# Output projection of a hybrid decoder layer by seven block products, with attention's turns spaced by a least amount of other matmuls

## The chip, the cores and the metric

One core of one Trainium2 chip runs the whole program. The time is that of the device, in microseconds (us), the median of the runs of one kernel. The profile and the trace come from one more execution, whose own time stands beside its span in the table below.

## The reference

One layer over 1024 tokens and 1024 channels in fp32: a combined projection, differential attention, an mLSTM, two gated merges, an output projection and a norm. What the change touches is the end:

```python
merged = (jax.nn.sigmoid(ga) * jnp.einsum('bsw,wd->bsd', ya, w_a[l])
          + jax.nn.sigmoid(gb) * jnp.einsum('bsw,wd->bsd', yb, w_b[l]))
out = jnp.einsum('bsd,de->bse', merged, w_out[l])
x = x + _rmsnorm(out, norm_post[l])
```

`ya` is the result of attention (4 heads, 8 query blocks of 128 each, causal), `yb` that of the mLSTM.

## The kernel before

**Precision.** A product of fp32 matrices is done in three passes of the type fp32r. `split` writes each operand as a high half (a copy by ScalarE, ACT, in which the type is narrowed) and a low half (`tensor_sub` on VectorE, DVE), and TensorE (PE) adds high by high, high by low and low by high. A product over 512 rows of depth and 512 columns is 4 times 3 = 12 matmuls of 128x512.

**Seven products in place of eight.** The projections at the start take a pair of column blocks. Inputs and weights are cut in two by two, and `Combos` and `Banks` make the four output blocks out of seven products (`PRODS`, products 0 to 6) of sums and differences of blocks. `pair_steps` gives the order: product 6 of a pair comes after product 0 of the next. `prep` makes the operand two products ahead, `run` issues 12 matmuls and then what follows (`after`): a copy to SBUF by ACT after products 0, 2 and 3, a finished block (`sink`) after products 1, 4, 5 and 6. The output projection does not use this scheme.

**Attention and the fill.** `attn_head` makes, for query block i, the scores (`score`, tile S), the exponentials (L956) and the difference of the two softmaxes (`combine`, L970) on DVE and ACT. In the next turn the result is transposed on PE (`turn`, tile pT), and a turn later weighed (`weigh`, tile pv). Between turns `weave` pulls other matmuls from `fill` (the remaining pairs, then the merge of the mLSTM's half, `merge_b`), six at a time, an amount of 1.4 in its own count. What a turn may pull is the supply over the turns by `share`, and what was pulled too much before is held back, though never below 0.6 of the want.

**Second merge and output projection.** `merge("ma", ...)` runs 16 groups of 12 matmuls (8 blocks d of columns, two halves of the tokens). After each group DVE multiplies by the gate out of PSUM (L1108), adds the other merge's result (L1181), and `split` writes M, high and low. Then come 16 output tiles of 24 matmuls (two column halves `cc`, eight token blocks `tt`). After each tile ACT squares it (L1209) and DVE multiplies by the norm's weights (L1213); in the second half each token block is finished by GpSimd (L1220, L1221), DVE (L1226) and a DMA out (L1230). The raw output weights are loaded and split by `out_weights` between the groups of the merges.

**What sets the order.** Each engine runs its own instructions in a fixed order. A scheduler orders them when the program is built; only the matmuls, up to the end of attention (L1169), are held to the order of the code. All DMAs are issued from SP, in one order. Tiles live in pools with few buffers (`raw` 4, `wc` 3, `st` 5, `tm` 4; PSUM 3 in `acc` and 5 in `misc`), and a tile waits until the last reader of the one before it is done.

Of the kernel before, what the change touches and what calls it, by code (L numbers as in the profile page):

```python
# [9 lines left out]
F32 = mybir.dt.float32  # L10
# [6 lines left out]
P = 128  # L17
# [16 lines left out]
RESERVE = 12.0  # L34
FB = 8
LAST = 5


@with_exitstack
def kernel(  # L40
# [47 lines left out]
    def acc(name):  # L88
        return ps_acc.tile([P, 512], F32, tag="acc", name=name)
# [4 lines left out]
    def slot(i, shape, name, dtype=F32):  # L94
        return tp.tile(shape, dtype, tag=f"T{i}", name=name)
# [7 lines left out]
    def raw_tile(shape, name):  # L103
        return wp.tile(shape, F32, tag="raw", name=f"raw_{name}", bufs=4)
# [4 lines left out]
    def drain(gen):  # L109
        for _ in gen:  # L110
            pass
# [226 lines left out]
    class Banks:  # L338


        def __init__(self, width, name, sink):
            self.w, self.name, self.sink = width, name, sink
            self.b, self.t = {}, {}

        def bank(self, b):
            if b not in self.b:
                self.b[b] = acc(f"{self.name}{b}")[:, 0 : self.w]
            return self.b[b]

        def keep(self, what, b):  # L350
# [684 lines left out]

    left = [0.0]

    def weave(chain):
        for want in chain:
            turns(2)  # L1040
            due = left[0] + want
            now = max(due, 0.6 * want)
            left[0] = pull(now) + due - now

    def until(name):
# [3 lines left out]
        left[0] -= pulled[0] - was  # L1049


    wide, homes = {}, {}

    def out_weights(cc, kh, g):

        if (cc, kh) not in homes:
            tags = {(0, 0): ("t4h", "t4l"), (1, 0): ("t2h", "t2l"), (1, 1): ("t1h", "t1l")}
            if (cc, kh) in tags:
                two = [
                    hp.tile([P, 4, 512], F32R, tag=f"h{t}", name=f"wo{t}") for t in tags[cc, kh]  # L1060
                ]
                homes[cc, kh] = [[two[e][:, n * 2 : n * 2 + 2] for e in range(2)] for n in range(2)]
            else:
                four = [slot(8 + n, [P, 2, 512], f"wo{n}", F32R) for n in range(4)]
                homes[cc, kh] = [four[0:2], four[2:4]]
        dst = homes[cc, kh][g]
        for k in range(2):
            for e in range(2):
                wide[cc, kh, g * 2 + k, e] = dst[e][:, k]
        r = raw_tile([P, 2, 512], f"o{cc}{kh}{g}")  # L1070
        k0 = kh * 4 + g * 2
        nc.sync.dma_start(r, w_out_v[:, k0 : k0 + 2, cc * 512 : cc * 512 + 512])
        split(r, *dst)


    def load_y(slot0, heads, tags):
# [42 lines left out]
    def merge_b():  # L1119
        ys = load_y(4, range(4), ("11h", "11l", "21h", "21l"))  # L1120
        n = 0
        for due in merge("mb", w_b_v, 1, ys, keep_b):
            yield due
            n += 1
            if n in (8, 14):
                out_weights(0, 0, (n - 8) // 6)
            if n == 20:
                ys_a.extend(load_y(0, range(3), YA))
        done.add("mb")
# [39 lines left out]
    ordered[0] = False  # L1169

    M = {}
    for kh in range(2):
        for T in range(2):
            for e in range(2):
                tag = (("t3h", "t3l"), ("22h", "22l"), ("21h", "21l"), ("11h", "11l"))[kh * 2 + T][e]
                M[kh, T, e] = hp.tile([P, 4, 512], F32R, tag=f"h{tag}", name=f"m{kh}{T}{e}")

    def finish_a(d, half, tg):
        mb = part("mb")
        nc.sync.dma_start(mb, m_d[d][:, hs_(half)])  # L1180
        nc.vector.tensor_add(tg, tg, mb)  # L1181
        split(tg, M[d // 4, half, 0][:, d % 4], M[d // 4, half, 1][:, d % 4])

    drain(merge("ma", w_a_v, 0, ys_a, finish_a, (acc, misc)))


    npost = slot(13, [P, D], "npost")
    nc.sync.dma_start(npost, norm_post[0].partition_broadcast(P))
    orow = [slot(i, [P, D], f"o_{i}") for i in range(8)]
    ssq = cp.tile([P, NT, 2], F32, name="ssq")  # L1190

    for cc in range(2):
        for kh in range(2):
            for g in range(2):
                if (cc, kh) != (0, 0):
                    out_weights(cc, kh, g)
        c0 = cc * 512
        for tt in range(NT):
            ts_ = slice(tt * P, (tt + 1) * P)
            js = slice((tt % 4) * P, (tt % 4 + 1) * P)  # L1200
            ps = (misc if tt % 2 else acc)("out")
            for kt in range(KT):
                for i, (a, b) in enumerate(((0, 0), (0, 1), (1, 0))):
                    mm(
                        ps, M[kt // 4, tt // 4, a][:, kt % 4, js], wide[cc, kt // 4, kt % 4, b],
                        start=(kt == 0 and i == 0), stop=(kt == KT - 1 and i == 2),
                    )
            junk = part("oj")
            nc.scalar.activation(  # L1209
                junk, ps, AF.Square, scale=D ** -0.5, accum_out=ssq[:, tt, cc : cc + 1]  # L1210
            )
            orr = orow[tt]
            nc.vector.tensor_mul(orr[:, c0 : c0 + 512], ps, npost[:, c0 : c0 + 512])  # L1213
            if cc == 0:
                nc.gpsimd.tensor_scalar(
                    ssq[:, tt, 0:1], ssq[:, tt, 0:1], 1.0, 4.0 * EPS, ALU.mult, ALU.add
                )
                continue
            st = sp.tile([P, 3], F32, tag="ost", name="ost")
            nc.gpsimd.tensor_add(st[:, 0:1], ssq[:, tt, 0:1], ssq[:, tt, 1:2])  # L1220
            nc.gpsimd.tensor_tensor(st[:, 2:3], st[:, 0:1], mhalf[:, 0:1], ALU.pow)  # L1221
            xr = slot(8 + tt % 4, [P, D], "xr")
            nc.sync.dma_start(xr, x[0, ts_, :])
            for n0 in range(0, D, 512):
                ns = slice(n0, n0 + 512)
                nc.vector.scalar_tensor_tensor(  # L1226
                    out=orr[:, ns], in0=orr[:, ns], scalar=st[:, 2:3], in1=xr[:, ns],
                    op0=ALU.mult, op1=ALU.add,
                )
                nc.sync.dma_start(out[0, ts_, ns], orr[:, ns])  # L1230


_INS = ["x", "norm_pre", "norm_post", "w_in", "b_if", "conv_qk", "lambda_qk",
# [25 lines left out]
```

## Time and profile before

| | |
|---|---|
| median of 3 runs | 843.53 us (843.45 to 843.87) |
| the profiled execution's own time | 841.9 us |
| mean granted clock of PE | 0.999 |

The program in stretches, busy us of each engine (the windows view; the last two stretches stand in the prediction):

| stretch, us | PE | DVE | ACT | DMA share |
|---|---|---|---|---|
| 0 to 40, load and first projections | 38.40 | 30.05 | 24.85 | 0.75 |
| 40 to 375, projections with the mLSTM | 335.00 | 251.09 | 162.58 | 0.41 |
| 375 to 680, attention with fill | 301.86 | 217.27 | 179.45 | 0.54 |
| 680 to 702.3, end of the first merge | 22.30 | 10.56 | 3.64 | 0.65 |

The columns of a timeline row are start, duration, engine, line, operation, out<-in, shape and count; what stands in brackets is idle time ahead of it and what ended it. Matmuls overlap, so a row's duration is not the pace: the pace is the distance of the starts.

### The profile page before, as it was taken

The page shows a single profiled execution, that of the slowest core. Times are in us where ns is not written, and L with a number is a line of the kernel's source. Part 1 is how long each engine was busy: PE and PEld are TensorE (multiplying, and loading weights), DVE is VectorE, ACT ScalarE, POOL GpSimd, SP SyncE. Part 2 cuts the span into 40 slices and gives each one's busy share as a digit, 9 for nine tenths or more (in the row PEclk, how much of TensorE's full clock was granted, in tenths as well). Part 3 has the DMA queues.
Part 4 walks back from the last instruction along what each step waited for, and adds up shares of the span by engine and source line. Part 5 has one row for each costly group of instructions (what it writes and reads, how often), then busy time and mean ns, then how long its engine had stood idle before and what let it go on. Part 6 is the DMA issues. An engine that isn't in the chain of part 4 may idle for free.

```text
span 840.2 us, 12224 instructions
## 1 busy us (share of the span) xinstructions
PE 829.3 (99%) x4282; PEld 706.5 (84%) x4282; DVE 573.0 (68%) x1161; ACT 400.4 (48%) x892; POOL 36.5 (4%) x70
## 2 busy tenths in 40 slices
PE   9999999999999999999999999999999999999997
PEld 7998888888888888888888888788888888888885
DVE  6996969769659767568767875587587734981133
ACT  6663545444544544446655655466576521341110
POOL 1100000000000000010010000000100000000011
PEclk9999999999999999999999999999999999999999
DMA  7712441451542547266256426442666757830252
GB/s 238 216 40 70 101 151 51 138 163 51 176 143 83 174 146 231 89 208 202 92 161 228 126 74 204 139 162 75 224 208 229 271 184 263 295 105 1 101 200 101
DMA packets 100482, 128.44 MB, mean 153 GB/s; under 512 B 8666, under 2 KB 60098, under 8 KB 100420
## 3 DMA queue, kind: packets, MB, share of 16 engines
q1 hardware_dynamic: 100420, 127.66, 47.9%
q8 instruction: 34, 0.56, 0.3%
q14 instruction: 28, 0.23, 0.1%
HBM read 88.27 MB, written 39.35 MB: 152 GB/s over the span
## 4 chain that ended last, share of the span: by engine, by line
PE 95%; DMA 2%; DVE 1%; ACT 1%; issue 1%; SPq 0%; POOL 0%; DVEq 0%; POOLq 0%; ACTq 0%
PE out L80 10%; PE mrg L80 10%; PE tok L80 6%; PE S L80 4%; PE pv L80 4%; PE pT L83 2%; PE num L80 2%; PE qkb0Y L80 1%; PE g04Y L80 1%; PE g00Y L80 1%; PE za1Y L80 1%; PE g12Y L80 1%; PE g02Y L80 1%; PE zb0Y L80 1%; PE za0Y L80 1%; PE g10Y L80 1%
## 5 line engine op out<-in xcount | busy, mean ns | idle before, releaser
L956 ACT ACTIVATE p<-p,ast 128x128 f32<-128x128 f32 (+7 forms) x64 | 49.5, 775 | 31.2 <-DVE ast L955 23.5
L949 DVE CUSTOM_DVE_ANT_0 p<-S,gm 128x384 f32<-128x384 f32 (+5 forms) x96 | 49.8, 554 | 13.4 <-PE S L80 11.7
L1213 DVE TENSOR_TENSOR o<-out,npost 128x512 f32<-128x512 f32 x16 | 11.1, 691 | 57.3 <-ACT oj L1209 57.3
L80 PE MATMUL mrg<-y,mbw 128*128 128x512 f32 x192 | 44.9, 391 | 0.0
L80 PE MATMUL mrg<-y,maw 128*128 128x512 f32 x192 | 43.7, 389 | 0.0
L1209 ACT ACTIVATE oj<-out 128x512 f32<-128x512 f32 x16 | 9.6, 598 | 71.5 <-PE out L80 71.5
L80 PEld LDWEIGHTS mrg<-y,maw 128*128 128x128 f32 x192 | 36.0, 188 | 7.5
L80 PEld LDWEIGHTS mrg<-y,mbw 128*128 128x128 f32 x192 | 35.8, 188 | 7.3
L80 PEld LDWEIGHTS pv<-va,pT 128*128 128x128 f32 x288 | 37.2, 191 | 2.6
L80 PE MATMUL pv<-va,pT 128*128 128x128 f32 x288 | 37.4, 275 | 0.0
L80 PE MATMUL S<-khh,qs 128*128 128x384 f32 (+5 forms) x96 | 34.9, 369 | 0.3 <-ACT pT L986 0.2
L80 PE MATMUL S<-kll,qs 128*128 128x384 f32 (+5 forms) x96 | 32.4, 342 | 0.4 <-DMA kll<-qk_d 0.4
L1108 DVE SCALAR_TENSOR_TENSOR tg<-tg,mrg 128x512 f32<-128x512 f32 x32 | 21.8, 682 | 14.6 <-PE mrg L80 12.9
L754 DVE SCALAR_TENSOR_TENSOR cv<-pad,cols,cv 128x1024 f32<-128x1024 f32 x24 | 30.7, 1280 | 0.2
L970 DVE SCALAR_TENSOR_TENSOR p<-p,ast,p 128x128 f32<-128x128 f32 (+7 forms) x32 | 26.1, 816 | 0.7
L823 ACT ACTIVATE junk<-raw 128x128 bf16<-128x128 f32 x32 | 9.9, 310 | 31.6 <-DVE raw L818 31.4
L80 PE MATMUL out<-wo,m 128*128 128x512 f32 x96 | 23.7, 395 | 0.0
L83 PE MATMUL pT<-ident,p 128*128 128x128 f32 x144 | 21.2, 274 | 2.5 <-DVE p L970 2.5
L986 ACT COPY pT<-pT 128x512 f32<-128x512 f32 (+3 forms) x48 | 21.9, 488 | 2.7 <-PE pT L83 2.5
L80 PEld LDWEIGHTS out<-wo,m 128*128 128x128 f32 x96 | 18.0, 188 | 4.4 <-DVE m L115 0.2
L995 ACT ACTIVATE oa<-pv 128x128 f32<-128x128 f32 x32 | 8.8, 276 | 26.3 <-PE pv L80 26.1
L80 PE MATMUL out<-wot4h,m 128*128 128x512 f32 x64 | 21.1, 390 | 0.0
(1240 smaller groups left out, 2465.4 us busy)
## 6 DMA issues: line engine op xcount, KB each, us to landing
raw_g<-in_w_in_dram SPq DMA_DIRECT2D x16, 512.0 KB, 3.6
g_d<-g SPq DMA_DIRECT2D x32, 256.0 KB, 3.6
tg<-g_d SPq DMA_DIRECT2D x32, 256.0 KB, 3.5
raw_qkb<-in_w_in_dram SPq DMA_DIRECT2D x16, 256.0 KB, 3.2
z_d<-zt SPq DMA_DIRECT2D x16, 256.0 KB, 2.8
zs<-z_d SPq DMA_DIRECT2D x16, 256.0 KB, 4.6
raw_qka<-in_w_in_dram SPq DMA_DIRECT2D x16, 256.0 KB, 3.1
qk_d<-qah SPq DMA_DIRECT2D x16, 256.0 KB, 2.3
```

The source lines that it names most:

```text
L80: pin(nc.tensor.matmul(*args, **kw))
L83: pin(nc.tensor.transpose(out=out, in_=in_, identity=ident))
L754: nc.vector.scalar_tensor_tensor(out=cv, in0=pad[:, t : t + S], scalar=cols[:, t * 8 + blk : t * 8 + blk + 1], in1=cv, op0=ALU.mult, op1=A ...
L823: nc.scalar.activation(junk, raw[:, c, 0:P], AF.Square, accum_out=stbs[h, c // 4][:, 1, c % 4 : c % 4 + 1])
L949: nc.vector.tensor_tensor_reduce(out=pr[:, n0:n1], in0=pss[:, : n1 - n0], in1=gm[:, (7 - i) * P + n0 : (7 - i) * P + n1], scale=-0.125, sc ...
L956: nc.scalar.activation(pr[:, :nk], pr[:, :nk], AF.Exp, bias=nm, scale=-1.0, accum_out=sth[:, c, i : i + 1],)
L970: nc.vector.scalar_tensor_tensor(out=p0[:, :nk], in0=p1[:, :nk], scalar=st[:, 3:4], in1=p0[:, :nk], op0=ALU.mult, op1=ALU.add,)
L986: nc.scalar.copy(pT[:, j0:j1], pt[:, 0 : (j1 - j0) * P].rearrange("p (j t) -> p j t", t=P))
L995: nc.scalar.activation(raw[:, i], pv[:, 0:P], AF.Square, accum_out=sth[:, 2, i : i + 1])
L1108: nc.vector.scalar_tensor_tensor(out=tg, in0=tg, scalar=1.0, in1=ps, op0=ALU.add, op1=ALU.mult)
L1209: nc.scalar.activation(junk, ps, AF.Square, scale=D ** -0.5, accum_out=ssq[:, tt, cc : cc + 1])
L1213: nc.vector.tensor_mul(orr[:, c0 : c0 + 512], ps, npost[:, c0 : c0 + 512])
```

## The change

Three parts.

**The output projection** is done by the seven-product scheme. Four pairs (`OutPair`, p = 0 to 3) take token blocks p and p + 4 and both column halves: 28 products of 12 matmuls in place of 16 tiles of 24. The weights' sums and differences (t1 to t4) and their halves are made by `wo_first` in steps between the groups of the second merge, the halves of block 22 and of t4 inside the first four products. M is kept in fp32 (`finish_a` adds straight into it), its combinations and halves are made per product by `prep`. A token block is finished (`finish_row`) as soon as both of its column halves are done, so during the products and not in a second pass.

**Attention's turns.** `weave` gets a least amount (CHAIN = 5.2) for attention: a turn pulls at least that much, or its whole want where that is less, whatever was pulled too much before.

**One pull of 2.5** ahead of the first head.

```diff
-    def weave(chain):
+    def weave(chain, least=0.0):
         for want in chain:
             turns(2)
             due = left[0] + want
-            now = max(due, 0.6 * want)
+            now = max(due, 0.6 * want, min(want, least))
             left[0] = pull(now) + due - now
...
     flip_half(*before[0], 7, 1)
+    pull(2.5)
...
-        weave(attn_head(h, stk, gm, supply, before if h else None, after, res))
+        weave(attn_head(h, stk, gm, supply, before if h else None, after, res), CHAIN)
...
     def finish_a(d, half, tg):
         mb = part("mb")
         nc.sync.dma_start(mb, m_d[d][:, hs_(half)])
-        nc.vector.tensor_add(tg, tg, mb)
-        split(tg, M[d // 4, half, 0][:, d % 4], M[d // 4, half, 1][:, d % 4])
+        nc.vector.tensor_add(M[d // 4, half][:, d % 4], tg, mb)
...
+    def wo_first(g):
+        b11, b12, b22, b21 = (
+            wo_load(kh, cc, g, home)
+            for kh, cc, home in ((0, 0, 10), (0, 1, 11), (1, 1, 12), (1, 0, 8 + g))
+        )
+        yield
+        wo_split("11", g, b11)
+        yield
+        nc.vector.tensor_sub(b12, b12, b11)
+        wo_split("t1", g, b12)
...
+    for n, _ in enumerate(merge("ma", w_a_v, 0, ys_a, finish_a, (acc, misc))):
+        if n % 2 and n > 2:
+            next(wo_steps, None)
...
+    class OutPair:
...
+        def early(self):
+            js = slice(self.p * P, self.p * P + P)
+            s2 = part(f"os2_{self.p}").rearrange("p (k c) -> p k c", k=4)
+            self.cb = Combos(M[0, 0][:, :, js], M[1, 0][:, :, js], M[0, 1][:, :, js], M[1, 1][:, :, js], s2)
...
+    for n, (p, i) in enumerate(steps):
+        if n + 2 < len(steps):
+            q, i2 = steps[n + 2]
+            outs[q].prep(i2)
+        if n == 0:
+            wo_home("22", ("t2h", "t2l"))
+            wo_home("t4", ("t1h", "t1l"))
+        if n in (0, 1):
+            wo_split("22", n, wo_load(1, 1, n))
+        if n in (2, 3):
+            wo_split("t4", n - 2, t4_raw[n - 2])
+        outs[p].run(i)
```

How the orders change, at three places. **PE, start of attention's third head**, before: from the last scores of block 0 (S) to their transpose (pT); qka3 is a projection pair of the fill.

```order
L80 MATMUL S<-kll_2_5258,qs_2_5254 128x128
L80 MATMUL qka3Y<-ht2h,qka3w_5315 128x512
L80 MATMUL qka3Y<-ht2l,qka3w_5315 128x512
L80 MATMUL qka3Y<-ht2h,qka3w_5315 128x512 x2
L80 MATMUL qka3Y<-ht2l,qka3w_5315 128x512
L80 MATMUL qka3Y<-ht2h,qka3w_5315 128x512
L80 MATMUL qka3Z<-ht1h,qka3w_5361 128x512
L80 MATMUL qka3Z<-ht1l,qka3w_5361 128x512
L80 MATMUL qka3Z<-ht1h,qka3w_5361 128x512 x2
L80 MATMUL qka3Z<-ht1l,qka3w_5361 128x512
L80 MATMUL qka3Z<-ht1h,qka3w_5361 128x512
L83 MATMUL pT<-ident,p_5415 128x128
```

The same engine and turn now; between the S rows and the first of these stand four more matmuls of qka3Z.

```order
L81 MATMUL qka3Z<-ht1l,qka3w_5361 128x512
L81 MATMUL qka3Z<-ht1h,qka3w_5361 128x512
L81 MATMUL qka3Y<-ht3h,qka3w_5397 128x512
L81 MATMUL qka3Y<-ht3l,qka3w_5397 128x512
L81 MATMUL qka3Y<-ht3h,qka3w_5397 128x512 x2
L81 MATMUL qka3Y<-ht3l,qka3w_5397 128x512
L81 MATMUL qka3Y<-ht3h,qka3w_5397 128x512 x2
L81 MATMUL qka3Y<-ht3l,qka3w_5397 128x512
L81 MATMUL qka3Y<-ht3h,qka3w_5397 128x512 x2
L81 MATMUL qka3Y<-ht3l,qka3w_5397 128x512
L81 MATMUL qka3Y<-ht3h,qka3w_5397 128x512
L84 MATMUL pT<-ident,p_5434 128x128
```

18 matmuls stand between scores and transpose, where there were 12. **DVE, from the last groups of the second merge (tg<-tg,mrg) into the output projection**, before:

```order
L1108 SCALAR_TENSOR_TENSOR tg<-tg,mrg 128x512
L1181 TENSOR_TENSOR tg<-tg,mb 128x512
L115 TENSOR_TENSOR wot2l<-raw_o_7594,wot2h 128x1024
L1108 SCALAR_TENSOR_TENSOR tg<-tg,mrg 128x512
L115 TENSOR_TENSOR m_6966<-tg,m_6965 128x512
L1181 TENSOR_TENSOR tg<-tg,mb 128x512
L115 TENSOR_TENSOR wot2l<-raw_o_7598,wot2h 128x1024
L115 TENSOR_TENSOR m_6968<-tg,m_6967 128x512
```

The same place now; the two tg<-tg,mrg are again the last two groups, m_6953 and m_6954 are the lower halves of M in depth, ow is the operand of a product, os its combination s2, wo22 and wot4 are halves of the output weights.

```order
L1140 SCALAR_TENSOR_TENSOR tg<-tg,mrg 128x512
L1209 TENSOR_TENSOR m_6953<-tg,mb 128x512
L116 TENSOR_TENSOR wo22l<-raw_o_7371,wo22h 128x1024
L1140 SCALAR_TENSOR_TENSOR tg<-tg,mrg 128x512
L116 TENSOR_TENSOR ow_7359<-m_6953,ow_7359 128x512
L1209 TENSOR_TENSOR m_6954<-tg,mb 128x512
L116 TENSOR_TENSOR wo22l<-raw_o_7394,wo22h 128x1024
L329 TENSOR_TENSOR os_0_7352<-m_6954,m_6952 128x512
L116 TENSOR_TENSOR wot4l<-o_7014,wot4h 128x1024
L116 TENSOR_TENSOR ow_7362<-os_0_7352,ow_7362 128x512
```

The operand of product 1 (ow_7359) stands right behind the last group, that of product 2 (ow_7362) five instructions further, two of them of 128x1024. **DVE, end of pair 0**, before: a token block in the second pass of the projection.

```order
L1213 TENSOR_TENSOR o_7339<-out,npost 128x512
L1226 SCALAR_TENSOR_TENSOR o_7339<-o_7339,ost,xr 128x512 x2
L1213 TENSOR_TENSOR o_7340<-out,npost 128x512
L1226 SCALAR_TENSOR_TENSOR o_7340<-o_7340,ost,xr 128x512 x2
```

Now, from the sink of product 5 of pair 0 to the sink of product 6:

```order
L1253 TENSOR_TENSOR o_7411<-out_u_7434,out0Z 128x512
L116 TENSOR_TENSOR ow_7506<-m_6953,ow_7506 128x512
L329 TENSOR_TENSOR os_1_7353<-m_6954,m_6952 128x512
L1258 TENSOR_TENSOR o_7411<-o_7411,npost 128x512
L1238 SCALAR_TENSOR_TENSOR o_7411<-o_7411,ost,raw_xr_7500 128x512 x2
L334 TENSOR_TENSOR m_6951<-os_1_7353,m_6951 128x4x128
L116 TENSOR_TENSOR ow_7524<-os_1_7353,ow_7524 128x512
L336 TENSOR_TENSOR m_6953<-m_6953,os_1_7353 128x4x128
L1258 TENSOR_TENSOR o_7472<-out0Y,npost 128x512
L1238 SCALAR_TENSOR_TENSOR o_7472<-o_7472,ost,raw_xr_7547 128x512 x2
```

Operands of pair 1 now stand between the sinks of pair 0, behind instructions that wait for products and for GpSimd.

More of the change, by code (lines that the diff above doesn't have):

```diff
@@ L36 @@
 LAST = 5
+CHAIN = 5.2
 @with_exitstack
@@ L1049, in until @@
         left[0] -= pulled[0] - was
[L1052 to L1070, printed above, removed]
+    WO = {}
@@ new lines, in wo_home, with wo_slots, wo_split @@
+    def wo_home(name, tags):
+        two = [hp.tile([P, 4, 512], F32R, tag=f"h{t}", name=f"wo{name}{e}") for t, e in zip(tags, "hl")]
+        WO[name] = [[two[e][:, g * 2 : g * 2 + 2] for g in range(2)] for e in range(2)]
+    def wo_slots(name, first_):
+        WO[name] = [
+            [slot(first_ + e * 2 + g, [P, 2, 512], f"wo{name}{e}{g}", F32R) for g in range(2)]
+            for e in range(2)
+        ]
+    def wo_split(name, g, raw):
+        split(raw, WO[name][0][g], WO[name][1][g])
@@ L1187 @@
+    drain(wo_steps)
     npost = slot(13, [P, D], "npost")
     nc.sync.dma_start(npost, norm_post[0].partition_broadcast(P))
-    orow = [slot(i, [P, D], f"o_{i}") for i in range(8)]
     ssq = cp.tile([P, NT, 2], F32, name="ssq")
[L1192 to L1207, printed above, removed]
+    orow, ocount = {}, {}
@@ L1217 @@
                 )
[L1218 to L1230, printed above, removed]
+            else:
+                finish_row(tt)
```

101 lines of the change are left out of this document (86 added, 15 removed).

## The prediction

> **What bounds the kernel now.** I read the page's busy times and chain first, then the chain in order of time, then the waits of PE.
>
> ```profile
> span 840.2 us, 12224 instructions
> ...
> PE 829.3 (99%) x4282; PEld 706.5 (84%) x4282; DVE 573.0 (68%) x1161; ACT 400.4 (48%) x892; POOL 36.5 (4%) x70
> ...
> PE 95%; DMA 2%; DVE 1%; ACT 1%; issue 1%; SPq 0%; POOL 0%; DVEq 0%; POOLq 0%; ACTq 0%
> ```
>
> PE is busy nearly throughout and is 95% of the chain: a matmul less is time less, as long as DVE and ACT keep up. The chain in order of time ends with these rows; the first is a single product of the projections:
>
> ```profile
> 482.79 2.72 PE qka2Y L80 x12
> ...
> 691.82 54.43 PE mrg L80 x240
> 746.25 87.83 PE out L80 x384
> ```
>
> A matmul of 128x512 takes 2.72/12 = 0.227 us in a product and 54.43/240 = 0.227 in the merge; the output projection runs at 87.83/384 = 0.229. It holds 87.83 us and nothing else is in its chain. Whether the other engines have room is read from the windows of the second merge and of the projection:
>
> ```profile
> core 0: us, PE busy (x) PEld busy (x) DVE busy (x) ACT busy (x) POOL busy (x), PEclk, DMA share, GB/s
> 702.30:746.10 43.80, 43.80 (x195) 36.25 (x195) 32.80 (x50) 13.32 (x21) 0.00 (x0) 1.00 0.79 263
> 746.10:834.10 88.00, 87.97 (x385) 71.81 (x383) 29.17 (x41) 15.88 (x37) 7.02 (x22) 1.00 0.25 90
> ```
>
> In the projection DVE has 59 us free; in the merge 11, and the change loads both.
>
> **The projection's matmuls.** 28 products of 12 replace 384 matmuls. At 2.72 us, a few at 2.73, they take 76.3 us, so 87.83 - 76.3 = **11.5 us** go. The operands that PE reads are still halves of type fp32r (the rows ow, wo), so I keep the pace. The Trainium skill ("TensorE: Matmul & The Clock Gate", Back-to-back issue gap) gives about 131 ns as the sustained distance of matmuls with 512 columns; by it the 48 matmuls that go would be worth 6.3 us. The trace's own 227 ns speaks against it, and the measurement decides.
>
> **Attention.** The waits view gives PE two real waits there, and the timeline shows the first as start to start:
>
> ```profile
> PE pT L83 <- DVE p L970: 2.5, 2, 1.5
> PE S L80 <- DMA kll<-qk_d: 0.4, 1, 0.4
> ```
>
> ```profile
> 541.41 0.28 PE L80 MATMUL S<-kll,qs 128*128 128x128 f32 x1
> ...
> 544.10 0.39 PE L80 MATMUL qka3Z<-ht1h,qka3w 128*128 128x512 f32 x1
> 545.94 0.30 PE L83 MATMUL pT<-ident,p 128*128 128x128 f32 x1 [1.45 <-DVE p L970]
> ...
> 550.35 0.47 PE L80 MATMUL qka3Y<-ht3h,qka3w 128*128 128x512 f32 x1
> 551.85 0.44 PE L83 MATMUL pT<-ident,p 128*128 128x128 f32 x2 [1.02 <-DVE p L970]
> ```
>
> From 544.10 to 545.94 PE did one matmul of 0.23: 1.6 us lost; from 550.35 to 551.85, 1.3. The busy view hides 0.2 of each, since ends are modelled. In the new order 18 matmuls stand where 12 did, 1.36 us more, which leaves some 0.2 of the first wait; the second gets at least as much and goes. That is 2.7 us. The kll wait gets 2.8 us of matmuls (the pull of 2.5) ahead of it: up to 0.4 more. Against it, turns late in a head now pull four sixes where they pulled up to six. The longest chain of such a turn, block 7 of head 0:
>
> ```profile
> 421.37 0.48 PE L80 MATMUL S<-khh,qs 128*128 128x512 f32 x1
> ...
> 423.07 0.39 PE L80 MATMUL S<-kll,qs 128*128 128x512 f32 x1
> ...
> 428.74 1.28 DVE L970 SCALAR_TENSOR_TENSOR p<-p,ast,p 128x1024 f32<-128x1024 f32 x1
> ...
> 431.49 1.73 PE L80 MATMUL pv<-va,pT 128*128 128x128 f32 x14
> ...
> 433.05 1.04 PE L83 MATMUL pT<-ident,p 128*128 128x128 f32 x8
> ```
>
> The scores end at 423.3 and p at 430.0, 6.7 us; PE used 9.7 us there. Four sixes and the seven weighings (431.49 to 433.05, 1.56) now give 24 x 0.227 + 1.56 = 7.0 us: just enough here, too little where DVE is held by other work. I take 0.5 us for such turns, between 0 and 2.9, today's two waits coming back. Attention: **-2.6 us**, between -3.1 and +0.2.
>
> **The hand-over to the projection.** DVE's durations, and ACT's casts:
>
> ```profile
> L1108 DVE SCALAR_TENSOR_TENSOR tg<-tg,mrg 128x512 f32<-128x512 f32 x21 | 14.3, 681 | 5.7 <-PE mrg L80 4.5 <-DMA tg<-g_d 1.2
> L1226 DVE SCALAR_TENSOR_TENSOR o<-o,ost,xr 128x512 f32<-128x512 f32 x16 | 11.3, 748 | 1.8 <-POOL ost L1221 1.8
> L115 DVE TENSOR_TENSOR m<-tg,m 128x512 fp32r<-128x512 f32 x16 | 11.0, 690 | 4.7 <-ACT m L114 4.1
> L1181 DVE TENSOR_TENSOR tg<-tg,mb 128x512 f32<-128x512 f32 x16 | 11.0, 687 | 0.2
> L115 DVE TENSOR_TENSOR wo<-raw_o,wo 128x1024 fp32r<-128x1024 f32 x2 | 2.5, 1225 | 4.7 <-ACT wo L114 4.7
> ...
> L114 ACT CAST m<-tg 128x512 fp32r<-128x512 f32 x16 | 9.9, 622 | 23.1 <-DVE tg L1181 23.0
> ```
>
> Fp32 M saves DVE 16 x 0.69 = 11 us in the merge; against it come 18 instructions of 128x1024 at 1.22 (five halves and four differences for each of two parts), 22 us, of which some five run ahead of it. From the merge's first group to its last the new order has 15 multiplies, 15 adds, 11 others of 128x512 and 12 of 128x1024 on DVE. Back to back, starts are 0.08 less apart than durations (746.85 to 747.46 below for 0.69): 41 x 0.61 + 12 x 1.14 = 39 us, against 15 x 2.72 = 40.8 on PE. That leaves no room to catch up once DVE is late, and it is late today:
>
> ```profile
> 711.85 1.23 DVE L115 TENSOR_TENSOR wo<-raw_o,wo 128x1024 fp32r<-128x1024 f32 x1 [4.66 <-ACT wo L114]
> ...
> 746.85 0.69 DVE L115 TENSOR_TENSOR m<-tg,m 128x512 fp32r<-128x512 f32 x1 [0.69 <-ACT m L114]
> 747.46 0.68 DVE L1108 SCALAR_TENSOR_TENSOR tg<-tg,mrg 128x512 f32<-128x512 f32 x1
> ...
> 749.92 0.68 DVE L1108 SCALAR_TENSOR_TENSOR tg<-tg,mrg 128x512 f32<-128x512 f32 x1
> ```
>
> The merge's matmuls end at 746.3, DVE takes up the last group at 749.9: 3.6 us late since a load of weights held it for 4.7. Today that costs PE nothing. In the new order, with DVE late by L, the operand of product 2 is ready L + 5.4 after PE ends the merge (multiply, low half, add, weights 1.14, combination, weights 1.14, low half: 5 x 0.62 + 2 x 1.14), and PE wants it, after two products and two matmuls, at 5.9. The weights of the second half are again loaded late (slot 10 comes free only when the first half is used). I take L = 3: **+2.5 us**, between 0 (L up to 0.5) and 5 (L = 5.5, half more than today).
>
> **Inside the pairs.** Per pair DVE does 11 instructions for operands, 3 adds and 4 multiplies at 0.69 and 4 of L1226 at 0.75: 15.4 us, and PE takes 7 x 2.72 = 19.0. After each finished block DVE waits for ACT's square and GpSimd, today's rows at the end showing 1.6 us from the square to L1226, of which the multiply covers 0.7: 15.4 + 2 x 0.9 = 17.2. That fits; **+0.3 us** for single late operands, between 0 and 2.
>
> **The end.**
>
> ```profile
> 831.13 6.43 SPq L1230 DMA_DIRECT2D out_dram<-o  x4
> ...
> 833.68 0.39 PE L80 MATMUL out<-wot1h,m 128*128 128x512 f32 x1
> ...
> 834.17 0.60 ACT L1209 ACTIVATE oj<-out 128x512 f32<-128x512 f32 x1 [4.75 <-PE out L80]
> ...
> 835.79 1.41 DVE L1226 SCALAR_TENSOR_TENSOR o<-o,ost,xr 128x512 f32<-128x512 f32 x2 [0.21 <-POOL ost L1221]
> ```
>
> The block before the last now ends one product, 2.7 us, before the end instead of 5.5; its L1226 still stands ahead of the last multiply: **+0.2 us**, between 0 and 1.
>
> **Sum.** -11.5 - 2.6 + 2.5 + 0.3 + 0.2 = **-11.1 us**. The profiled execution took 841.9 (span 840.2 and 1.7 around it), so its like would take 830.8. The median of the runs is 843.53, 1.6 above it; from there I predict **832.4 us**.
>
> **Rivals.**
>
> *The hand-over holds PE for long.* For it: DVE at 39 of 40.8 us, and 4.7 us lost today to one load. With 5 us there instead of 2.5 the time is 835. And PE has a slow pace, seen at the start of the program:
>
> ```profile
> 14.93 1.08 PE L80 MATMUL tok<-wc,h21l 128*128 128x264 f32 x4
> 15.81 0.83 PE L80 MATMUL tok<-wc,h21h 128*128 128x264 f32 x4
> 16.48 0.64 PE L80 MATMUL tok<-wc,h11h 128*128 128x256 f32 x4
> 16.96 0.27 PE L83 MATMUL xT<-ident,x 128*128 128x128 f32 x1
> ```
>
> Four matmuls of 264 columns took 0.88 us until 15.8, four of 256 then 0.48: nearly double pace. If a wait threw PE back to the slow pace for some 12 matmuls, 12 x 0.23 = 2.7 us come on top: 837.6, in round numbers 838. Against it: the product behind the wait that ends at 551.85 keeps its pace.
>
> ```profile
> 554.13 2.73 PE qka3Z L80 x12
> ```
>
> The clock gate of the Trainium skill ("TensorE: Matmul & The Clock Gate", What's actually happening) halves the clock after an idle window of about 3.4 us; no wait of PE in this trace is so long after the start, so the runs so far cannot show it. **15%, 838.**
>
> *The waits of attention move.* Late turns have less cover: by the upper bound above +0.2 instead of -2.6, so 835. For it: 7.0 us of cover against a chain of 6.7. Against it: the same turns then also hold less of the fill's DVE work. **12%.**
>
> *DVE paces the pairs: slower than before.* Its FIFO puts each operand behind a sink. Today the low half of M waits 0.69 us for its cast in many groups (the row with 4.7 idle). If all 7 operands of a pair waited so, and all 4 sinks 0.9, a pair takes 15.4 + 4.8 + 3.6 = 23.8 us, and the projection 95.2 + 2.5 against 87.8: 851. It ends slower than today from 22.6 us a pair (3.5 more than PE's 19.0, 14 us in four pairs). Against it: the order puts operands two products ahead, so casts mostly run beside other DVE work. **5%.**
>
> *The products do not save what they should*, because matmuls lose pace with new tiles: nothing in the order speaks for it; 843.5. **2%.**
>
> *Everything fits*: -11.5 for the matmuls, -3.1 in attention, no late hand-over: 829. **7%.**
>
> **How the numbers follow.** My forecast has 59%; its own range is 830 to 835. The range for 8 in 10 is 828.5 to 838.5: left out are the DVE rival, the one without a saving and the far ends of the others. A measurement of this kernel tells about 0.2% from no change. Faster by more: 59 + 15 + 12 + 7 = 93%; within: 2%; slower: 5%.
>
> **What would show it.** The chain's rows of out3 should end about 76 us plus waits after the second merge; out rows x336 at 0.227. PE's waits for p L973 should be below 1 us in sum, and those late in heads show whether they moved. At the hand-over, the distance from the last merge matmul to the last multiply on DVE is L, and gaps of PE before products 1 and 2 are its price. I am wrong if PE's gaps inside the pairs exceed 2 us, if the merge itself waits for weights, or if attention's gaps are as large as before.

## The result, and the profile after

The changed kernel takes **833.0 us** (median of 4 runs, 832.1 to 834.2) where the kernel before, in the runs beside it, took 843.5: a ratio of 0.9891, with a 95% interval of 0.9877 to 0.9904. Measured once more later, beside other kernels, it stood at 0.9861 (0.9835 to 0.9887). The profiled execution took 832.5 us where that of before took 841.9, so 9.4 less. The ratios below, though not the medians, leave out one of nine executions of the kernel with two more multiplies per product: the profiled one, which took 2747 us, so that this kernel has no usable profile.

The page of the changed kernel, the rows that answer to those of before (span, busy time by engine, shares of the chain that ended last):

```profile
span 830.8 us, 12221 instructions
...
PE 817.1 (98%) x4234; PEld 696.6 (84%) x4234; DVE 613.6 (74%) x1215; ACT 420.5 (51%) x922; POOL 45.8 (6%) x70
...
PE 83%; DVE 6%; DMA 5%; issue 3%; ACT 1%; SPq 1%; POOL 0%; DVEq 0%; ACTq 0%; POOLq 0%
```

48 matmul records are gone, PE is busy 12.2 us less and DVE 40.6 us more, and PE's share of the chain has dropped from 95% to 83%: DVE and DMAs now end last in places. That is not a measure of lost time, as PE is still busy 98% of the span. Where PE stood still, its waits say (what waited and for what, us in all, times, the longest; waits of the program's start left out):

```profile
PE pT L84 <- DVE p L973: 1.6, 1, 1.6
...
PE qka1Z L81 <- ACT qka_p L355: 1.1, 1, 1.1
PE mrg L81 <- DVE maw L116: 1.0, 1, 1.0
...
PE out0Y L81 <- ACT ow L115: 0.4, 1, 0.4
...
PE out0Y L81 <- DVE ow L116: 0.3, 1, 0.3
...
PE mrg L81 <- DVE tg L1140: 0.2, 1, 0.2
```

The two waits for p of before (2.5 us) and the one for kll (0.4) are gone. In their place stand two others in attention, and two inside the merges (mrg), for which the prediction's sum has no term.

The hand-over, in the timeline of the changed kernel:

```profile
734.86 10.72 PE L81 MATMUL mrg<-y,maw 128*128 128x512 f32 x46 [0.96 <-DVE maw L116]
745.42 0.39 PE L81 MATMUL out0Y<-wo11h,ow 128*128 128x512 f32 x1
...
747.46 0.68 DVE L1140 SCALAR_TENSOR_TENSOR tg<-tg,mrg 128x512 f32<-128x512 f32 x1
...
751.84 0.50 PE L81 MATMUL out0Y<-wot2h,ow 128*128 128x512 f32 x1 [0.45 <-ACT ow L115]
752.13 0.68 DVE L116 TENSOR_TENSOR ow<-os,ow 128x512 fp32r<-128x512 f32 x1
...
752.87 0.73 PE L81 MATMUL out0Y<-wot2h,ow 128*128 128x512 f32 x2 [0.30 <-DVE ow L116]
```

PE goes over to the projection at 745.42. DVE takes up the last group of the merge at 747.46, so 2.0 us late, and the operand of product 2 is complete at 752.13 + 0.68 = 752.8; PE's matmul that reads its low half starts at 752.87. From there to the end the chain is products without a gap; four rows of it, the products 2 to 5 of the last pair, and the window of the second pair:

```profile
810.34 2.72 PE out3Y L81 x12
813.06 2.79 PE out3Z L81 x12
815.85 2.79 PE out3Y L81 x12
818.64 2.76 PE out3Z L81 x12
```

```profile
core 0: us, PE busy (x) PEld busy (x) DVE busy (x) ACT busy (x) POOL busy (x), PEclk, DMA share, GB/s
764.60:783.70 19.10, 19.10 (x85) 15.67 (x84) 13.74 (x21) 8.61 (x19) 3.86 (x6) 1.00 0.32 112
```

The stage ends with the last matmul at 824.1, and DVE then finishes the last two token blocks, of which these rows are the start:

```profile
823.72 0.39 PE L81 MATMUL out3Y<-wot4h,ow 128*128 128x512 f32 x1
...
824.31 1.42 DVE L1238 SCALAR_TENSOR_TENSOR o<-o,ost,raw_xr 128x512 f32<-128x512 f32 x2 [0.71 <-POOL ost L1233]
...
825.65 0.68 DVE L1258 TENSOR_TENSOR o<-out3Y,npost 128x512 f32<-128x512 f32 x1
```

So the projection takes 824.1 - 745.4 = 78.7 us. Before, counted in the same way, from the first matmul to the end of the last, it took 88.0 (746.1 to 834.1), so 9.3 less. The rest of the 9.4 cancels: the program's start is 0.9 shorter and the stretch from there to the second merge 1.0, the second merge is 1.2 longer and the end 0.6.

### The profile page after: what moved, and what is told of

Read it like the earlier page. It is cut to its first block, busy times and chain, and to the rows that moved or that the text cites. A ratio compares the mean times of both kernels' runs of the same rounds, so it can differ in the third digit from the quotient of the medians.

```text
span 830.8 us, 12221 instructions
## 1 busy us (share of the span) xinstructions
PE 817.1 (98%) x4234; PEld 696.6 (84%) x4234; DVE 613.6 (74%) x1215; ACT 420.5 (51%) x922; POOL 45.8 (6%) x70
## 4 chain that ended last, share of the span: by engine, by line
PE 83%; DVE 6%; DMA 5%; issue 3%; ACT 1%; SPq 1%; POOL 0%; DVEq 0%; ACTq 0%; POOLq 0%
PE tok L81 6%; PE S L81 4%; PE pv L81 3%; PE pT L84 2%; PE num L81 2%; DVE tg L1140 1%; PE qkb0Y L81 1%; PE za1Y L81 1%; PE g04Y L81 1%; PE g12Y L81 1%; PE g02Y L81 1%; PE g00Y L81 1%; PE g06Y L81 1%; PE zb0Y L81 1%; PE g10Y L81 1%
## 5 line engine op out<-in xcount | busy, mean ns | idle before, releaser
L115 ACT CAST ow<-m 128x512 fp32r<-128x512 f32 x24 | 14.8, 621 | 20.1 <-PE mrg L81 2.4
L116 DVE TENSOR_TENSOR ow<-m,ow 128x512 fp32r<-128x512 f32 x24 | 16.4, 688 | 10.2 <-ACT ow L115 10.2
L583 DVE SCALAR_TENSOR_TENSOR y<-yT,cols,zs 128x512 f32<-128x512 f32 x16 | 12.0, 748 | 10.8 <-DMA zs<-z_d 10.2
L81 PEld LDWEIGHTS S<-khh,qs 128*128 128x128 f32 x96 | 18.1, 188 | 1.8 <-ACT pT L989 0.4
L545 ACT ACTIVATE g<-g 128x512 f32<-128x512 f32 x24 | 15.1, 630 | 8.0 <-DVE g L544 5.6
```

The lines of the kernel that those rows point to most:

```text
L81: pin(nc.tensor.matmul(*args, **kw))
L115: nc.scalar.copy(hi, raw)
L116: nc.vector.tensor_sub(lo, raw, hi.bitcast(F32))
L545: nc.scalar.activation(st, bank if kept is None else st, AF.Tanh, scale=0.5)
L583: nc.vector.scalar_tensor_tensor(out=y, in0=pt, scalar=ncol, in1=zs, op0=ALU.mult, op1=ALU.mult)
```

## The experiments

Each kernel was timed in turns with the kernel before; the ratio is what counts, as the time of the kernel before differed between the groups of runs by 1 us. The first four, the next four and the last four shared their runs.

| kernel | median, us | before beside it | ratio (95%) |
|---|---|---|---|
| output projection alone | 834.94 | 841.93 | 0.9912 (0.9890 to 0.9934) |
| attention parts alone | 840.79 | 841.93 | 0.9978 (0.9962 to 0.9994) |
| without the pull of 2.5 | 833.90 | 841.93 | 0.9895 (0.9870 to 0.9920) |
| splits behind the operands | 831.85 | 841.93 | 0.9872 (0.9847 to 0.9897) |
| raw tiles freed early | 830.75 | 841.78 | 0.9869 (0.9847 to 0.9890) |
| one more multiply per product | 833.19 | 841.78 | 0.9885 (0.9862 to 0.9908) |
| splits behind, copy first | 833.15 | 841.78 | 0.9888 (0.9858 to 0.9918) |
| the same, t3 later | 827.36 | 841.78 | 0.9827 (0.9806 to 0.9849) |
| the changed kernel again | 832.17 | 842.72 | 0.9861 (0.9835 to 0.9887) |
| t3 later, load_y at 26 | 829.93 | 842.72 | 0.9840 (0.9815 to 0.9866) |
| t3 later, load_y at 14 | 829.13 | 842.72 | 0.9828 (0.9804 to 0.9852) |
| two more multiplies per product | 847.43 | 842.72 | 1.0049 (1.0025 to 1.0072) |

**The parts of the change, each alone.** First the projection without the attention parts:

```diff
-    pull(2.5)
...
-        weave(attn_head(h, stk, gm, supply, before if h else None, after, res), CHAIN)
+        weave(attn_head(h, stk, gm, supply, before if h else None, after, res))
```

> The changed kernel without its two attention parts (no least amount, no pull of 2.5). Theory: the output projection carries most of the gain. The prediction's terms for it are -11.5 + 2.5 + 0.3 + 0.2 = -8.5 us against the kernel before (835.0); the trace of the changed kernel gives -9.1 for the projection (87.83 to 78.7), +1.1 for a new wait in the second merge and +0.6 at the end, so -7.4 (836.1). Its PE waits for p L973 should be as before: 1.6 and 1.3 us. Rival: the attention parts gave nothing, waits only moved: then 833.0, no different from the changed kernel.

Then the kernel before with these two edits and nothing else:

> The kernel before with the two attention parts alone; the output projection stays at 16 tiles of 24 matmuls. Theory: -2.6 us by the prediction (840.9), -1.9 by what the changed kernel's trace shows (841.6): the waits of 1.6 and 1.3 us for p and the kll wait go, and one wait of 1.25 us (a product of qka1 for ACT's copy) and one of 1.7 us late in head 3 come. Rival: the waits only move, within 0.5 us of 843.5.

The projection alone gives 0.9912, so -7.4 us of 841.9; attention alone 0.9978, so -1.9 (between -3.2 and -0.5). Together that is -9.3, where the change gives -9.2 by its first ratio and -11.7 by its second: within the intervals the parts add up, and most of the gain is the projection's. The waits view of the projection alone has the old waits for p again, four of them where before had two:

```profile
PE pT L84 <- DVE p L973: 4.2, 4, 1.5
```

With attention alone there is a single wait in attention, late in head 3, but it is long, and something comes behind it. Its timeline row, and the stretch behind it in the windows view (the last three columns are granted clock, DMA share and GB/s):

```profile
657.83 0.87 PE L84 MATMUL pT<-ident,p 128*128 128x128 f32 x6 [2.12 <-DVE p L971]
```

```profile
659.16:662.57 3.41, 3.41 (x10) 2.91 (x9) 1.97 (x8) 1.36 (x3) 0.00 (x0) 0.50 0.68 232
```

After a wait of 2.12 us PE ran at half its clock for 3.4 us, which is 1.7 us lost beside the wait: the slow pace of the prediction's first rival, met in attention and not at the hand-over.

**Without the pull of 2.5** (the line taken out of the changed kernel, the least amount kept):

> The changed kernel without the pull of 2.5 ahead of the first head; the least amount stays. Theory A: the pull moves the products of qka1 ahead, so the new wait of 1.25 us near 388 us is its price and the wait for kll (0.58 us) its gain: without it 0.6 us less, 832.4. Theory B: the least amount makes the wait near 388 us: it stays, and the kll wait comes back, 0.6 us more, 833.6.

Its ratio cannot be told from the changed kernel's. The kll wait comes back in its profile (0.7 us), and near 388 us a wait for ACT stays, for another copy of the same pair:

```profile
388.18 0.50 PE L81 MATMUL qka1Y<-ht3h,qka1w 128*128 128x512 f32 x1 [1.89 <-ACT qka_u L355]
```

So theory A falls. Theory B is not proven by it either: most kernels further down have the changed kernel's own order up to there, and in their profiles the wait near 388 is between nothing and 1.9 us. The order only leaves room for it; how long it is differs from one profile to the next (its cause stands in the section on the prediction).

**The splits at the hand-over.** The halves of block 22 and of t4 are put behind the operand just prepared, on DVE and ACT, as an order of issue without a wait:

```diff
+    def split_behind(name, g, raw):
+        v, s = last_on(nc.vector.engine), last_on(nc.scalar.engine)
+        with tc.issue_after(v), tc.issue_after(s):
+            wo_split(name, g, raw)
...
-            wo_split("22", n, wo_load(1, 1, n))
+            split_behind("22", n, wo_load(1, 1, n))
...
-            wo_split("t4", n - 2, t4_raw[n - 2])
+            split_behind("t4", n - 2, t4_raw[n - 2])
```

> The changed kernel with the splits of block 22 and t4 held behind the operand of the product prepared just before, on DVE and ACT (issue order only). Theory: PE's 1.4 us of gaps at the hand-over (748.4 to 753) come from two splits of wo22 and one of t4, 1.14 us each, ahead of the operands of products 1 and 2: without them the operand of product 2 is ready at about 751.4 and PE loses 0.1 to 0.3, so 1.2 us less, 831.8. Rival: the lateness that DVE brings from the second merge sets it, and waits for ACT take the place of the splits: 0 to 0.4 us less.

In its timeline:

```profile
750.21 0.62 ACT L115 CAST ow<-os 128x512 fp32r<-128x512 f32 x1 [2.88 <-DVE os L329]
750.73 1.04 ACT L115 CAST wo22h<-raw_o 128x1024 fp32r<-128x1024 f32 x1
751.68 0.58 ACT L355 COPY out_p<-out0Y 128x512 f32<-128x512 f32 x1
...
752.31 0.50 PE L81 MATMUL out0Y<-wot2h,ow 128*128 128x512 f32 x1 [1.09 <-ACT out_p L355]
```

By this trace the rival was right, though the ratio alone could not tell: the wait is nearly as long as before (1.4 us by PE's starts, 1.65 in the changed kernel) and has another name. Product 2 adds into the bank that product 0 wrote, so it needs ACT's copy of product 0 too, and that copy now stands behind the cast of block 22. The next kernel issues the copy first (`run(0)` ahead of the operand of product 2, whose cast is held behind the copy):

```diff
+        if n == 0:
+            outs[p].run(i)
...
+            if n == 0:
+                with tc.issue_after(last_on(nc.scalar.engine)):
+                    outs[q].prep(i2)
```

> As the kernel in which the splits of block 22 and t4 are held behind the operands, but with ACT's copy of product 0 ahead of its cast for product 2's operand. There PE lost 1.25 us at product 2, waiting for that copy. Theory: with the copy first it waits for the operand alone, which is ready 0.1 to 0.4 us late: 1.0 us less than the changed kernel, 832.0. Rival: the operand is late by as much as the copy was, DVE being 2 us late from the merge: the gap stays at 1.0 to 1.3.

Now PE waits for nothing at the hand-over; the waits view of this kernel has no row of the projection at all. Yet the time is that of the changed kernel. In the profiled execution a longer wait in the second merge, with a drop of the clock behind it, took the gain back:

```profile
736.28 6.00 PE L81 MATMUL mrg<-y,maw 128*128 128x512 f32 x18 [2.73 <-DVE maw L116]
```

```profile
733.09:736.50 3.41, 0.68 (x4) 0.26 (x3) 3.41 (x6) 0.62 (x1) 0.00 (x0) 1.00 0.76 268
736.50:739.91 3.41, 3.41 (x9) 2.62 (x9) 3.41 (x6) 0.00 (x0) 0.00 (x0) 0.50 0.53 172
```

This is not the wait of the hand-over in another place, since DVE's order up to there is that of the changed kernel. What differs is when a load of the second part of the weights lets DVE go on, in the changed kernel and then in this one:

```profile
718.97 1.23 DVE L1089 TENSOR_TENSOR o<-o,o 128x1024 f32<-128x1024 f32 x1 [1.38 <-DMA o<-in_w_out_dram]
```

```profile
720.38 1.23 DVE L1089 TENSOR_TENSOR o<-o,o 128x1024 f32<-128x1024 f32 x1 [4.24 <-DMA o<-in_w_out_dram]
```

The first is 18.3 us behind the first matmul of the second merge, the second 20.1. In the six profiles with this order (the changed kernel's two, this one, and those without the pull, with the splits behind and with one more multiply) that distance lies between 17.9 and 20.1, and PE's wait for maw, 0.5 to 2.7 us, is each time the distance less 17.4.

**What makes DVE late in the merge.** One kernel changes only the order in which the raw tiles are read, so that the second part's weights can be loaded earlier:

```diff
-        nc.vector.tensor_sub(b11, b22, b11)
-        wo_split("t3", g, b11)
-        yield
         wo_split("21", g, b21)
         yield
         nc.vector.tensor_sub(b21, b21, b22)
         t4_raw.append(b21)
+        nc.vector.tensor_sub(b11, b22, b11)
+        yield
+        wo_split("t3", g, b11)
```

> The changed kernel with the split of block 21 and the difference for t4 made ahead of those for t3 in each part of the weights, so that the raw tiles come free earlier for the second part's loads. Theory: DVE's lateness in the second merge, and with it the wait of 1.1 to 1.8 us for maw at 733, come from the late loads of the second part (DVE sat idle 1.4 us for one and then had four instructions of 1.22 us in a row of ten): that idle time goes, the wait falls below 0.3, DVE is at most 1 us late at the last group, and the time is 1.3 us less than the changed kernel's, 831.7. Rival: it is the amount of DVE's work between two groups that makes it late; then the wait stays within 0.4 us.

The forecast fails. The edit did not do what it was made for: in its timeline DVE's idle time for the load is 2.8 us, and the load ends no earlier (18.9 us behind the merge's first matmul). In its waits view the wait for maw is gone, but the hand-over costs more, 2.4 us in place of 0.7:

```profile
716.56 1.22 DVE L1089 TENSOR_TENSOR o<-o,o 128x1024 f32<-128x1024 f32 x1 [2.79 <-DMA o<-in_w_out_dram]
```

```profile
PE out0X L81 <- DVE ow L116: 0.9, 1, 0.9
PE out0X L81 <- ACT ow L115: 0.7, 1, 0.7
PE out0Y L81 <- ACT ow L115: 0.5, 1, 0.5
...
PE out0Y L81 <- DVE ow L116: 0.3, 1, 0.3
```

So a new theory: given when the load lands, it is the amount of work that DVE has between the second part's load and the first products. It is paid for either at maw or at the hand-over, and it goes only if work leaves this stretch or the load comes earlier; no run here makes the load earlier. The second part's t3 (a difference and a split) and its difference for t4, three instructions of 1.14 us, move behind the operands of the first products:

```diff
+    def t3_last():
+        nc.vector.tensor_sub(held[0], held[1], held[0])
+        wo_split("t3", 1, held[0])
+    def t4_last():
+        nc.vector.tensor_sub(held[2], held[2], held[1])
+        wo_split("t4", 1, held[2])
...
+        if n == 0:
+            behind(t3_last)
+        if n in (1, 2):
+            behind(lambda: wo_split("22", n - 1, wo_load(1, 1, n - 1)))
+        if n == 3:
+            behind(lambda: wo_split("t4", 0, t4_raw[0]))
+        if n == 4:
+            behind(t4_last)
```

> As that kernel, with the second part's t3 (difference and split) and difference for t4 moved out of the second merge to behind the operands of the first products: 3 times 1.14 = 3.4 us less for DVE in the merge. Theory: DVE then keeps up with the merge, the wait for maw at 733 (1.1 to 1.8 us) and the hand-over's 1.4 us both fall below 0.4: 2.0 us less than the changed kernel, 831.0, and faster than either kernel. Rival: the work moved holds up operands or the sinks' tiles in the first pair: a gap of 1 us or more there takes half of it back.

This is the fastest kernel: 0.9827, 827.4 us. In its timeline and windows:

```profile
716.60 1.22 DVE L1097 TENSOR_TENSOR o<-o,o 128x1024 f32<-128x1024 f32 x1 [4.36 <-DMA o<-in_w_out_dram]
...
740.67 0.39 PE L81 MATMUL out0Y<-wo11h,ow 128*128 128x512 f32 x1
...
742.13 0.68 DVE L1152 SCALAR_TENSOR_TENSOR tg<-tg,mrg 128x512 f32<-128x512 f32 x1
```

```profile
702.00:741.50 39.50, 39.50 (x176) 32.72 (x175) 34.29 (x49) 7.37 (x11) 0.00 (x0) 1.00 0.81 279
740.67:817.69 77.02, 77.02 (x337) 62.87 (x335) 59.63 (x88) 37.57 (x74) 17.11 (x22) 1.00 0.24 82
```

DVE was idle 4.4 us for the same load, which ended 19.4 us behind the merge's first matmul; in the changed kernel's order that would be a wait of 2.1 us. PE lost nothing, neither in the second merge nor in the projection. DVE is 742.13 - 740.67 = 1.5 us late, and that now fits. Against the changed kernel this is 3 to 5 us by the two ratios of that kernel. From the first matmul of the second merge to the end of the last product its profile takes 120.5 us; that of the changed kernel takes 123.5, of the splits behind the operands 123.9, of the raw tiles freed early 124.1 and of the copy first 125.2. In those four the loss stands at maw, at the hand-over or at both; here 2.9 us of the changed kernel's are gone, and what the ratios have beyond that lies within the intervals.

**How much DVE work the pairs can take.** The changed kernel with one more multiply per product, and with two:

```diff
+        spare = part("oj")
+        nc.vector.tensor_mul(spare, npost[:, 0:512], npost[:, 512:1024])
         outs[p].run(i)
```

> The changed kernel with one more multiply of 128x512 on DVE per product of the output projection, into a spare tile: 28 times 0.61 = 17 us of DVE work, 4.3 per pair. By the prediction's 17.2 us a pair it is then 21.5 against PE's 19.0: 10 us more in all, 843. By DVE's busy time in the changed kernel (57.4 of 78.7 us, 13.9 a pair) it is 18.2, which still fits: 0 to 1 us more, 833 to 834. With the prediction's waits for ACT and GpSimd (1.8) on top of that busy time 20.0: 4 us more, 837.

> The changed kernel with two more multiplies of 128x512 on DVE per product: 56 times 0.61 = 34 us, 8.5 per pair. One more per product cost nothing that could be measured, so DVE's own work is nearer to 13.9 us a pair (its busy time) than to the prediction's 17.2. By 13.9 a pair now takes 22.4 against PE's 19.0: 13.7 us more than the changed kernel, 846 to 847; with 1.8 of waits for ACT and GpSimd 24.2, so 21 us more, 854. Rival: DVE was far from its limit and even this fits: 833 to 836.

The first costs nothing that can be measured. Its window of the second pair:

```profile
762.40:781.60 19.20, 19.20 (x86) 15.76 (x85) 17.96 (x29) 8.54 (x19) 6.17 (x6) 1.00 0.33 110
```

DVE is busy 18.0 of 19.2 us and PE never waits. The second has no usable profile, so what follows is worked out and not read from a trace. It makes the kernel 13 to 16 us slower than the changed one (by its two ratios), 3.3 to 4.0 per pair, so that a pair takes some 22.5 to 23.2 us. If DVE paces the pairs there, its own need is that less 8.5 for the added work, 14.0 to 14.7 per pair, and not 17.2; the window of the changed kernel above has 13.7 busy.

**Attention's late wait.** The changed kernel again, and the kernel with t3 later with `load_y` asked for at other places (`n == 26` or `n == 14` in place of 20), on the same chip:

> The changed kernel once more, beside the three that follow on the same chip. Theory: its single waits (1.25 us at 388, 1.7 us at 655, 1.1 us at 733) depend on when DMAs land and differ from one execution to the next, while the hand-over's 1.3 to 1.4 us stays: ratio to the kernel before 0.988 to 0.990. Rival: they belong to the order and come back within 0.2 us.

> The kernel with t3 later, with the loads of attention's first three results (load_y) asked for after 26 steps of the first merge in place of 20. On ACT the third of their casts then stands behind the exponentials of block 5, no longer ahead of them. Theory: PE's wait for p late in head 3 (1.0 us there, 0.4 to 2.3 in the other runs) falls below 0.3, so 0.5 to 1 us less than with t3 later alone, 826.5. Rival: the wait passes to block 6 or to the start of the second merge, which needs those tiles: no gain.

> The same, with the loads asked for after 14 steps. All three casts then stand about one block earlier, two of them between the two exponentials of block 4. Theory: the wait leaves block 5, but block 4 can wait now, for loads that are issued just before: within 0.5 us of the kernel with t3 later. Rival: loads asked for earlier have landed when ACT comes to them: 0.5 to 1 us less.

In the repeat the waits moved within one program, as expected: at maw 0.5 in place of 1.0 us, late in head 3 0.8 in place of 1.6, near 388 1.9 in place of 1.1, with a half clock behind it; at the end of the first merge PE waited 1.5 us for DVE (tg) in place of 0.2. The hand-over had 0.8 as against 0.7. Its timeline and window:

```profile
391.56 0.50 PE L81 MATMUL qka1Z<-h22h,qka1w 128*128 128x512 f32 x1 [1.92 <-ACT qka_p L355]
```

```profile
392.04:395.46 3.42, 3.42 (x13) 2.92 (x12) 3.30 (x6) 1.70 (x6) 0.00 (x0) 0.50 0.00 0
```

With 26 the third cast stands behind the exponentials, but the second one stays ahead of them and waits 3.2 us for its load, and PE's wait only falls from 0.8 to 0.5 us; with 14 the wait is one block earlier, behind the second cast. The rows of the first, then of the second:

```profile
651.49 1.05 ACT L115 CAST y<-raw_yr 128x1024 fp32r<-128x1024 f32 x1 [3.19 <-DMA raw_yr<-y_d]
...
655.94 0.87 PE L84 MATMUL pT<-ident,p 128*128 128x128 f32 x6 [0.47 <-DVE p L973]
```

```profile
644.04 1.05 ACT L115 CAST y<-raw_yr 128x1024 fp32r<-128x1024 f32 x1 [1.02 <-DMA raw_yr<-y_d]
...
649.82 0.77 PE L84 MATMUL pT<-ident,p 128*128 128x128 f32 x5 [1.46 <-DVE p L973]
```

Neither is faster than t3 later alone. The wait comes from a cast that ACT, in its fixed order, meets before its load has landed, with the exponentials queued behind it; moving the loads moves the block that pays.

## Why the prediction was right, and where its steps were off

The time (832.4 against 833.0), the sign and the split hold: the projection's matmuls carry the gain, attention is small, and some of it is given back where DVE is late. The forecast case came in, none of the rivals. That it is only 0.6 us off is in part luck. The sum said 11.1 us; the profiled executions give 9.4, of which 0.9 is not the change (below), and the two ratios 9.2 and 11.7. And the median of before lay 1.6 us above its profiled execution, that of the changed kernel only 0.5. By its own terms, against the profiled execution:

- **The matmuls, -11.5: about -11.0.** The count of 28 products was right, the duration not quite. Product 2 takes 2.72 us, but 3 and 4 take 2.79 and 5 takes 2.76, so 19.2 a pair where the step had 19.0. In the kernel with t3 later, whose projection has no wait, the stage takes 77.0 us where before it took 88.0; the step had 76.3.
- **Attention, -2.6: -1.9 (between -3.2 and -0.5) by the part alone.** The old waits went as told. But the step took the new order's price from PE's cover alone (0.5 us for late turns), and the waits that came, 1.6 and 1.1 us in the changed kernel's profile, were of another kind: an engine in its fixed order meets an instruction whose load has not landed. Late in head 3 that is ACT's cast of y; near 388 us it is DVE's multiply with zs, with the casts, the exponentials and the copy that PE waits for behind it. Its rows in the changed kernel and in the repeat stand below. In seven profiles with this order DVE was idle there for 2.2 to 3.9 us, and PE waited 1.9 us less than that each time; in three it was idle for 1.8 us or less, and PE did not wait. The step named the bound of 2.9 for its waits, for another reason.
- **The hand-over, +2.5: the rule right, the place incomplete.** The rule was that the operand is ready L + 5.4 after PE ends the merge; measured L was 2.0, not 3, and the operand came 7.4 later (745.42 to 752.8). By that rule the wait is 1.5 us, and the starts of PE's rows lose 1.65 (0.7 of it seen as waits, since the rows' ends are modelled). What the step missed is that lateness is also paid inside the merge, where the weight's low half for the next block (maw) stands in DVE's queue: 1.0 us here, which makes the merge 1.2 longer, and 2.7 in another kernel. The step took L from the late load; but the load's lateness is paid at maw, and L was 2.0 in all four profiles with this hand-over, whatever the wait at maw. So L comes from DVE's work behind maw. The prediction had named a merge waiting for weights as a sign that it was wrong, and on this point it was. Both together are 2.9, so the term held by two errors that offset each other.
- **Inside the pairs, +0.3: nothing.** No gap of PE, and the room is larger than the step had: its 15.4 us added durations where starts are 0.08 closer, and added waits for ACT and GpSimd, while DVE's busy time is 13.7 us a pair. The rival in which DVE paces the pairs came true, as far as the time tells, only with two added multiplies per product; its limit of 22.6 us a pair, above which the kernel is slower than before, fits that run (22.5 to 23.2, and slower by 0.5%).
- **The end, +0.2: +0.6.** The last matmul ends 830.8 - 824.1 = 6.7 us before the end of the span, 6.1 before. The reason was the named one: L1238 of the block before (1.42 us) stands ahead of the last multiply.

About 0.9 us of the 9.4 is not the change. The same 48 matmuls of the program's start stand in the two chains, of before and then of after, at

```profile
47.66 5.74 PE tok L80 x48
```

```profile
46.77 5.74 PE tok L81 x48
```

so the profiled execution of after had a quicker start, with the same code. The rows on the multiply with zs, of the changed kernel and then of its repeat:

```profile
384.31 0.75 DVE L583 SCALAR_TENSOR_TENSOR y<-yT,cols,zs 128x512 f32<-128x512 f32 x1 [3.03 <-DMA zs<-z_d]
```

```profile
386.20 0.75 DVE L583 SCALAR_TENSOR_TENSOR y<-yT,cols,zs 128x512 f32<-128x512 f32 x1 [3.86 <-DMA zs<-z_d]
```

Of the rivals, the hand-over that holds PE and sets off the slow pace was not met by the changed kernel's profiled execution, but its mechanism is real (below), at 1.7 us for one drop where the prediction put 2.7.

What stays open: why the loads that DVE and ACT meet near 385, 650 and 718 us land at other times from one execution to the next; no run here shows what sets it. Open too is the wait for tg at the end of the first merge, 0.2 us here and up to 2.0 in another kernel's profile, which neither the prediction nor an experiment took up.

## What to carry to other kernels

When a change gives work to an engine that has room on average, add up that engine's work in the stretch between its last late input and the first moment that the bound engine needs its result: that sum decides, not the share of busy time. If a wait moves when it is removed at one place, as here from the splits to a copy, and from a merge's weights to the hand-over, the backlog is the cause; take work out of the stretch, as moving three instructions of 1.14 us did. Before a wait is called moved, look whether the late input itself came at another time. In an engine's fixed order, look at what stands ahead of the item that is waited for, and at whether its own input has landed.

## What the runs showed of the hardware

PE's clock drops after a shorter wait than the prediction reckoned with. Waits of 1.92, 2.12 and 2.73 us were each followed, within 1.4 us of their end, by 3.41 us at a granted clock of 0.50; a wait of 1.89 us, and those of 1.6 and less, were not. Each drop costs 1.7 us, so a wait of about two microseconds can nearly double its price.

Why 1.89 and 1.92 came out differently, the clock records of the traces show. After the start, the changes of the clock within one trace lie whole multiples of 3.413 us apart, and each drop began at the end of a stretch of this grid in which PE had stood still for 1.9 us or more. The wait of 1.89 us lay across the border of two stretches. Two such stretches, of the changed kernel's repeat, with the drop behind it, and of the kernel without the pull, with none:

```profile
388.63:392.04 3.41, 1.49 (x7) 0.94 (x6) 3.34 (x11) 2.39 (x9) 0.00 (x0) 1.00 0.59 223
```

```profile
386.49:389.90 3.41, 1.73 (x9) 1.46 (x10) 3.03 (x9) 3.16 (x9) 0.00 (x0) 1.00 0.76 289
```

PE stood still for 1.92 us of the first and 1.68 of the second, so the limit lies between the two in these traces; every other stretch after the start with 1.6 us idle or less was without a drop. The Trainium skill ("TensorE: Matmul & The Clock Gate", What's actually happening) puts the drop after at least one idle window of about 3.4 us. The 3.41 us agree with the length of that window, but a window idle for 1.92 us of it was enough here, and the measurement decides.
